# The start of an FFN's up projection: two operand copies moved from GpSimd to ScalarE, a new order of the last tile's steps, and the sample convolution cut into steps

## The chip, the cores and the metric

The kernel runs on one core of a Trainium2 chip. A core has five engines with a queue each: TensorE (PE, matrix products, with its weight loads shown as PEld), VectorE (DVE), ScalarE (ACT), GpSimd (POOL) and SyncE (SP, which only issues transfers here). They share an on-chip memory of 128 partitions (SBUF) and the accumulators that PE writes (PSUM). Each engine works through its own list in order and waits on semaphores for the others. The metric is the device time of one execution in microseconds; less is better.

## What is computed

One step of a one-layer hybrid encoder for 1024 prompt tokens and 32 sample tokens of a running stream, all in float32: a mixer with three kinds of heads, and behind it a feed-forward part with a short causal convolution. The change touches the first half of the feed-forward part.

```python
def causal_dwconv(x, buf, w, b):
    width, t = w.shape[0], x.shape[1]
    xp = jnp.concatenate([buf.astype(x.dtype), x], axis=1)
    y = b
    for j in range(width):
        y = y + xp[:, j:j + t] * w[j]
    return y, xp[:, t:]

def conv_ffn(xn, buf, w_up, conv_w, conv_b, w_down):
    up = xn @ w_up                                   # 1024 -> 2 * 2816
    up, buf = causal_dwconv(up, buf, conv_w, conv_b) # width 3
    gate, val = jnp.split(up, 2, axis=-1)
    return (jax.nn.gelu(gate, approximate=True) * val) @ w_down, buf

# in run_trunk, for the prompt and for the sample stream:
        x = x + rms_norm(h, g_mix_post[l])           # h: output projection of the mixer
        h, ffn_buf = conv_ffn(rms_norm(x, g_ffn_pre[l]), states[6][l], ffn_w_up[l], ffn_conv_w[l],
                              ffn_conv_b[l], ffn_w_down[l])
```

## The kernel before

**Products.** A float32 operand is kept as a high and a low half in PE's fp32r format, and each product is three matmuls, high x high, high x low and low x high (`mm3`, lines 88 to 90). The high half is made by an ACT cast, the low one by a DVE subtraction (`split`, line 94 and 97; `halves`, lines 1249 and 1250).

**Up projection.** The 22 feature tiles `f` hold 128 gate and 128 value columns each. A tile's product of 2 x 2 blocks (features x input rows against input rows x tokens) is done with seven block products instead of eight (`PROD`, `up_block`). Each goes with sums of weight blocks (A11, A12, A22 and S1 to S4, made for each tile by `up_operands`) and with sums of the normalised activations (B11, B21, B22, T1 to T4, made once by `col_operands`, from the blocks `xg` on lines 1258 to 1264, and kept for all tiles). A token block is 512 tokens wide. The results leave PSUM through ACT copies (`keep`, line 1333) and DVE sums into `uu` (line 1338); `up_finish` convolves `uu` (lines 1419 to 1425) and stores the product of both halves to `h_d`. Up to two tiles of `w_up` lie in `raw` buffers that the next loads reuse.

**The start.** The output projection of the mixer ends with token tiles 6 and 7 (`last[0]` and `last[1]`, generators of `outproj`). Their last steps, by `next`: add the norms' sums on POOL, scale, add the residual (DVE, lines 1167 to 1171), store, square (ACT, 1175), reciprocal root (POOL, 208 and 209), scale into `z` (ACT, 1178), and in the step behind it transpose `z` on PE (1195) and write it to `xg` with the column gains (DVE, 1199). Since these two tiles come late, tile 0 of the up projection is done in two halves: `s = 0` are the tokens of tiles 0, 1, 4 and 5, `s = 1` those of 2, 3, 6 and 7. The operands of `s = 0` are columns 0 to 255 of each operand tile, those of `s = 1` columns 256 to 511.

**Early places.** The tiles of T2 and T4 (pool `px1`) can only be laid where the output projection's weights (pool `p2`) have been. So T2 and T4 of `s = 0` are written first into the columns 256 to 511 of B22 and T1 (`early`), and copied to their own tiles afterwards by four instructions (line 1924). B22 and T1 of `s = 1` are written into the same columns behind these copies.

**Order.** A scheduler orders each engine's list by a simulated timeline and by priority, which is the order in which the instructions are issued in the code; `tc.high_priority(offset=n)` moves instructions up by `n` places. `with tc.issue_after(ins)` puts every instruction of the block that runs on the engine of `ins` behind `ins` in that engine's list. `kept` remembers instructions by name for this.

**Sample tokens.** The 32 sample tokens go through plain matmuls in 24 rounds of a 1 MB (for the last group 768 KB) load of `w_us` and 16 or 12 matmuls (`up_samples`, line 1452), in three groups of eight rounds with a transposition behind each group (lines 1463 and 1465). Two buffers `wus` take the loads. `up_all` steps this generator once for most tiles. The sample convolution (lines 1466 to 1476) runs on POOL on 128 x 704 elements, for the gate half into `smp_h` and for the value half into `smp_y`; its result is read only in the down projection.

**Pools.** Pools are stacked from both ends of SBUF: `px0` (B21, B11, T1, B22) on the left side, `p7` (`uu`, `fconv`, `pad1`, the `keep` tiles) and, opened after it and so next to it, `px1` (T3, T2, T4) on the right.

Of the kernel before, what the change touches and what calls it, by code (L numbers as in the profile page):

```python
# [8 lines left out]
F32 = mybir.dt.float32  # L9
# [3 lines left out]
AF = mybir.ActivationFunctionType  # L13
ALU = mybir.AluOpType
# [5 lines left out]
DEC = 32  # L20
# [58 lines left out]
def body(ctx: ExitStack, tc: tile.TileContext, a: dict):  # L79
# [988 lines left out]
    def outproj(p2, W, u):  # L1068
# [103 lines left out]
        sp.dma_start(x2_d[t0:t0 + n, :], x[:n])  # L1172
        if u == 7:
            z = tail[0]("z7")
        act.activation(z[:n], x[:n], AF.Square, accum_out=ss[:n, 0:1])
        rstd_of(ss[:n, 1:2], ss[:n, 0:1], n, 1, 1024)
        if u != 8:
            act.activation(z, x, AF.Copy, scale=ss[:, 1:2])
        else:
            dve.tensor_scalar(z[:n], x[:n], ss[:n, 1:2], None, op0=ALU.mult)  # L1180
        yield
# [49 lines left out]
    def col_operands(pool_, q, s, between=lambda: None, res=None, c=slice(None), parts="BTtq", at_=None):  # L1231

        res = {} if res is None else res
        q = {k: v[:, :, c] for k, v in q.items()}
        at = slice(256 * s + (c.start or 0), 256 * s + (c.stop or 256))

        def halves(name, src):
            if at_ and name in at_:
                h, l = at_[name]
            else:  # L1240
                if name not in res:
                    p = pool_[name in ("T2", "T4", "T3")]
                    res[name] = tuple(p.tile([128, 4, 512], F32R, name=f"{name}{x}") for x in "hl")
                h, l = (t[:, :, at] for t in res[name])
            with ExitStack() as late:
                if s == 0 and name in ("B21", "B11"):
                    late.enter_context(tc.issue_after(kept["ch"].ins))
                    late.enter_context(tc.issue_after(kept["cl"].ins))
                kept[name] = act.copy(h, src)
                return dve.tensor_tensor(l, src, h.bitcast(F32), op=ALU.subtract)  # L1250

        t1, t2, t3, t4 = q["B11"], q["B22"], q["B12"], q["B21"]
        if "B" in parts:
            halves("B21", t4)
            halves("B11", t1)
        if "T" in parts:
            between()
            dve.tensor_tensor(t1, t3, t1, op=ALU.subtract)
            halves("T1", t1)
            halves("B22", t2)  # L1260
        if "t" in parts:
            dve.tensor_tensor(t3, t2, t3, op=ALU.subtract)
            dve.tensor_tensor(t2, t2, t1, op=ALU.subtract)
            dve.tensor_tensor(t4, t2, t4, op=ALU.subtract)
            with ExitStack() as behind:
                if s == 0:
                    behind.enter_context(tc.issue_after(kept["jk"].ins))
                halves("T2", t2)
            kept["T4l"] = halves("T4", t4)
            between()  # L1270
        if "q" in parts:
            with tc.issue_after(kept["T4l"].ins), tc.issue_after(kept["T4"].ins), tc.issue_after(kept["T2"].ins):
                halves("T3", t3)
        return res
# [153 lines left out]
    def up_samples():  # L1428

        closing = ExitStack()  # L1430
        own = closing.enter_context(tc.tile_pool(name="pss", bufs=1, side="right", reuse_waits="tile"))

        def load(i):
            if i < len(ROUNDS):
                g, k = ROUNDS[i]
                nq = UGROUPS[g][1]
                sp.dma_start(wus[:, i % 2, :nq], a["w_us"][8 * g + k, :, :nq])

        smp_u = own.tile([128, NU, 2 + DEC], F32, name="smp_u")
        sp.dma_start(smp_u[:, :, 0:2], a["fcache"])  # L1440
        smp_y = [own.tile([128, NF, DEC], F32, name=f"smp_y{i}") for i in range(2)]
        smp_x = own.tile([128, 8, DEC], F32, name="smp_x")
        sp.dma_start(smp_x, xn_d[:, :, SEQ:])
        i = 0
        load(0)
        load(1)
        yield
        for g, (c0, nq) in enumerate(UGROUPS):
            ps = psf.tile([128, 512], F32, tag="sx", name=f"us{g}", bufs=1)
            for k in range(8):  # L1450
                for q in range(nq):
                    pe.matmul(ps[DEC * q:DEC * q + DEC], smp_x[:, k, :], wus[:, i % 2, q, :], start=k == 0, stop=k == 7)  # L1452
                load(i + 2)
                i += 1
                if k in (1, 3, 5):
                    yield
            m = DEC * nq
            us = own.tile([128, 512], F32, tag="us", name=f"usr{g}", bufs=1)
            act.copy(us[:m], ps[:m])
            yield  # L1460
            tp = psb.tile([128, 4, 128], F32, tag="big", name=f"ust{g}", bufs=3)
            for b in range(4):
                pe.transpose(tp[:, b, :m], us[:m, 128 * b:128 * b + 128], ident[:m, :m])
            for b in range(4):
                act.copy(smp_u[:, 4 * c0 + b:4 * (c0 + nq):4, 2:2 + DEC], tp[:, b, :m].rearrange("p (q t) -> p q t", t=DEC))
        pool.tensor_copy(fcq, smp_u[:, :, DEC:DEC + 2])
        for lo, dst in ((0, smp_h), (NF, smp_y[0])):
            js = slice(lo, lo + NF)
            w = [fconv[:, js, s:s + 1].broadcast_to([128, NF, DEC]) for s in range(4)]
            pool.tensor_tensor(dst, smp_u[:, js, 2:2 + DEC], w[2], op=ALU.mult)  # L1470
            pool.tensor_tensor(dst, dst, w[3], op=ALU.add)
            for s in range(2):
                pool.tensor_tensor(smp_y[1], smp_u[:, js, s:s + DEC], w[s], op=ALU.mult)
                pool.tensor_tensor(dst, dst, smp_y[1], op=ALU.add)
        act.activation(smp_h, smp_h, AF.Gelu_apprx_tanh)
        pool.tensor_tensor(smp_h, smp_h, smp_y[0], op=ALU.mult)
        closing.close()
        yield

    def up_all(pw_, W0, X, uus, py, freed, ahead, begun):  # L1480

        raw, W, summed = {}, {0: W0}, []
        late = None
        rounds = up_samples()
        n_rounds = 0
        for f in range(NF):
            uu = uus[f % len(uus)]
            if f + 1 < NF:
                raw[f + 1] = up_raw(f + 1)
            for s in (0, 1) if f == 0 else (None,):  # L1490
                if s != 0:
                    blk = up_block(pw_, f, s, W[f], X, uu)
                    next(blk)
                    next(late, None)
                    m = (2 * f + (1 if s is None else s) - 3) * len(SUMS) // 34
                    while len(summed) < min(m, len(SUMS)):
                        sum_weights(*SUMS[len(summed)])
                        summed.append(m)
                    if f:
                        up_finish(py(), f - 1, uus[(f - 1) % len(uus)])  # L1500
                        W.pop(f - 1)
                    next(blk)
                    if f == NF - 1:
                        freed()
                else:
                    blk = begun
                if s != 0 and f + 1 < NF:
                    ops = up_operands(f + 1, raw.pop(f + 1))
                    W[f + 1] = next(ops)
                    for _ in ops:  # L1510
                        pass
                yield
                while f and n_rounds < f * 15 // 17:
                    next(rounds, None)
                    n_rounds += 1
                next(blk)
                late = blk
                yield
        ahead()
        next(late, None)  # L1520
        up_finish(py(), NF - 1, uus[(NF - 1) % len(uus)])
# [2 lines left out]

    NP = NF // 2
    ROUNDS = [(g, k) for g in range(3) for k in range(8)]

    def sum_weights(t, n, q):

# [351 lines left out]
    uus[0] += [p7.tile([128, 2 + SEQ], F32, name=f"uu{j}") for j in range(2)]  # L1881
    for u in uus[0]:
        pool.memset(u[:, 0:2], 0.0)
    p7.tile([128, 8], F32, name="pad1")
    px1 = p8s.enter_context(tc.tile_pool(name="px1", bufs=1, side="right", reuse_waits="tile"))
    px.append(px1)
    col_operands(px, q0, 0, res=X, parts="q")
# [8 lines left out]
    wus = p3.tile([128, 2, 4, 512], F32, tag="xg0", name="wus", bufs=1)  # L1896
    py = []
    q1 = {f"B{k + 1}{j + 1}": (x1, xlate[1])[j][:, 4 * k:4 * k + 4, :] for k in range(2) for j in range(2)}
    with tc.high_priority(offset=10 * AHEAD), tc.issue_after(kept["T3"].ins):
        col_operands(px, q1, 1, res=X, parts="B")  # L1900
    with tc.high_priority(offset=10 * AHEAD):
        next(last[0])
        with tc.issue_after(kept["c1"].ins):
            next(last[1])
    begun = {}

    def freed():
# [11 lines left out]
    for i, _ in enumerate(up_all(pw_, W0, X, uus, lambda: py[0], freed, ahead, blk)):  # L1919
        if i == 1:  # L1920

            for n in ("T2", "T4"):
                for t, e in zip(X[n], early[n]):
                    pool.tensor_copy(t[:, :, :256], e)
            for x, c in zip(last, (slice(0, 128), slice(128, 256))):
                with tc.issue_after(done[0].ins), tc.issue_after(kept["c6"].ins):
                    next(x)
# [151 lines left out]
```

## Time and profile before

| | us |
|---|---|
| median of 3 runs | 1358.56 (1355.57 to 1362.2) |
| profiled execution | 1360.69 |
| its span | 1358.9 |
| PE busy | 1307.7 (96%) |
| DVE busy | 1018.0 (75%) |
| ACT busy | 693.8 (51%) |
| POOL busy | 316.2 (23%) |

A trace holds one execution; times in it count from the start of its span. A row of a timeline is start, duration, engine, line, operation, output tile <- input tiles, shapes and, in brackets, how long the engine had been idle and which instruction ended that. A row of the waits names who waited for whom, the sum, the count and the longest. A busy engine is not an engine at its peak: matmuls overlap, and the distance from one start to the next is what one costs. Tile 0 of the up projection runs from about 654 to 692 us, tile 21 ends near 1128.

### The profile page before, as it was taken

To read this page: it belongs to the slowest core of one execution; us is meant where nothing else is said; L and a number is where in the kernel's file an instruction comes from. 1 tells how busy PE (TensorE), PEld (TensorE's weight loads), DVE (VectorE), ACT (ScalarE), POOL (GpSimd) and SP (SyncE) were. 2 spreads that over 40 slices of the span, in tenths; PEclk is the share of its full clock that TensorE was granted. 3 is DMA by queue.
4 is the path that set the end of the run, shared out by engine and by line. 5 is a ranking of instruction groups with operands and counts; after the bars stand their busy time and mean duration, and the time that the engine had idled before them with its cause. 6 is when DMAs were issued, how large, how long until landed. Compare 5 with 4: busy or idle time off the path is not lost.

```text
span 1358.9 us, 25577 instructions
## 1 busy us (share of the span) xinstructions
PE 1307.7 (96%) x9896; PEld 1097.5 (81%) x9896; DVE 1018.0 (75%) x1748; ACT 693.8 (51%) x1294; POOL 316.2 (23%) x416
## 2 busy tenths in 40 slices
PE   6999999998999999999799999999999999999997
PEld 6999899998888977777788777877777886678885
DVE  5795659768598778865988777778789875399566
ACT  5555565464575556444555444544444444454552
POOL 4532312144031344232300101204023000010005
PEclk9999999999998999999999999999999999999999
DMA  9799879785889854444435888776864349644435
GB/s 342 241 356 368 275 242 286 267 284 180 295 253 326 307 202 131 145 144 159 128 129 171 236 246 220 199 220 184 243 157 116 102 159 358 242 159 131 148 111 123
DMA packets 134784, 291.73 MB, mean 215 GB/s; under 512 B 29015, under 2 KB 63991, under 8 KB 132535
## 3 DMA queue, kind: packets, MB, share of 16 engines
q1 hardware_dynamic: 121031, 267.03, 57.9%
q0 software_dynamic: 9120, 18.62, 7.6%
q10 hardware_dynamic: 4512, 4.46, 1.0%
q8 instruction: 77, 1.26, 0.4%
q14 instruction: 44, 0.36, 0.1%
HBM read 229.38 MB, written 85.78 MB: 232 GB/s over the span
## 4 chain that ended last, share of the span: by engine, by line
PE 57%; DVE 12%; ACT 3%; issue 2%; DMA 2%; POOL 1%; DVEq 0%; SPq 0%; POOLq 0%; ACTq 0%
PE pux_None L88 4%; PE pux_None L90 4%; PE pux_None L89 4%; PE puw_None L88 3%; PE puw_None L90 3%; PE puw_None L89 3%; PE q L88 2%; PE q L90 2%; PE q L89 2%; PE x L88 2%; PE x L89 2%; PE x L90 2%; PE us L1452 2%; PE zp L88 1%; PE zp L90 1%
## 5 line engine op out<-in xcount | busy, mean ns | idle before, releaser
L1422 DVE SCALAR_TENSOR_TENSOR y<-uu,fconv_sb,y 128x1024 f32<-128x1024 f32 x88 | 115.6, 1314 | 25.3 <-ACT y L1420 24.6
L1419 POOL COPY fhalo<-uu 128x2 f32<-128x2 f32 x44 | 17.6, 400 | 366.8 <-DVE uu L1338 355.0
L1420 ACT ACTIVATE y<-uu,fconv_sb 128x1024 f32<-128x1024 f32 x44 | 54.7, 1244 | 9.4 <-DVE uu L1338 8.9
L88 PE MATMUL pv<-wt_0h,xh 128*128 128x256 f32 (+1 forms) x192 | 56.5, 294 | 3.1 <-DVE xl L321 1.9
L90 PE MATMUL zp<-woh,cl 128*128 128x512 f32 (+1 forms) x144 | 57.6, 400 | 1.5 <-DVE cl L1093 1.5
L88 PE MATMUL zp<-woh,ch 128*128 128x512 f32 (+1 forms) x144 | 57.2, 406 | 0.8 <-ACT ch L1092 0.8
L89 PE MATMUL zp<-wol,ch 128*128 128x512 f32 (+1 forms) x144 | 57.6, 400 | 0.0
L90 PE MATMUL pv<-wt_1h,xl 128*128 128x256 f32 (+1 forms) x192 | 55.1, 287 | 0.0
L90 PE MATMUL pv<-wt_0h,xl 128*128 128x256 f32 (+1 forms) x192 | 54.9, 286 | 0.0
L88 PE MATMUL pv<-wt_1h,xh 128*128 128x256 f32 (+1 forms) x192 | 54.8, 286 | 0.0
L89 PE MATMUL pv<-wt_0l,xh 128*128 128x256 f32 (+1 forms) x192 | 54.7, 285 | 0.0
L89 PE MATMUL pv<-wt_1l,xh 128*128 128x256 f32 (+1 forms) x192 | 54.5, 284 | 0.0
L1655 POOL TENSOR_TENSOR gss<-gss 128x1 f32<-128x1 f32 (+1 forms) x9 | 9.2, 1021 | 186.8 <-ACT gjk L1648 186.8
L208 POOL TENSOR_SCALAR hrs<-hss 128x5 f32<-128x5 f32 (+3 forms) x27 | 10.1, 374 | 174.2 <-DVE hss L1002 169.6
L818 DVE COPY_PREDICATED P<-masks_sb,sc 128x352 f32<-128x352 int32 (+3 forms) x53 | 37.8, 714 | 5.8 <-PE sc L731 5.2
L88 PEld LDWEIGHTS pv<-wt_0h,xh 128*128 128x128 f32 x192 | 36.3, 189 | 5.3 <-DVE xl L321 2.4
L1424 ACT ACTIVATE y<-y 128x1024 f32<-128x1024 f32 x22 | 23.3, 1059 | 27.7 <-DVE y L1422 27.7
L88 PEld LDWEIGHTS pv<-wt_1h,xh 128*128 128x128 f32 x192 | 36.3, 189 | 0.7 <-issue 0.6
L209 POOL TENSOR_TENSOR hrs<-hrs,mhalf 128x5 f32<-128x5 f32 (+3 forms) x27 | 36.2, 1341 | 2.3
L89 PEld LDWEIGHTS pv<-wt_0l,xh 128*128 128x128 f32 x192 | 36.4, 190 | 0.2
L90 PEld LDWEIGHTS pv<-wt_0h,xl 128*128 128x128 f32 x192 | 36.4, 189 | 0.2
L90 PEld LDWEIGHTS pv<-wt_1h,xl 128*128 128x128 f32 x192 | 36.1, 188 | 0.3
(1898 smaller groups left out, 4679.0 us busy)
## 6 DMA issues: line engine op xcount, KB each, us to landing
wus<-in_w_us SPq DMA_DIRECT2D x16, 1024.0 KB, 6.5
wrP<-in_w_dn SPq DMA_DIRECT2D x27, 512.0 KB, 4.9
h_d<-y SPq DMA_DIRECT2D x22, 512.0 KB, 5.8
ht<-h_d SPq DMA_DIRECT2D x22, 512.0 KB, 9.5
wt_0r<-in_w_tok SPq DMA_DIRECT2D x21, 512.0 KB, 5.3
wt_1r<-in_w_tok SPq DMA_DIRECT2D x21, 512.0 KB, 6.1
ws_d<-in_w_dn POOLq DMA_DIRECT2D x20, 512.0 KB, 7.2
wrP<-ws_d SPq DMA_DIRECT2D x20, 512.0 KB, 4.1
```

Of the source, the lines that this page charges most:

```text
L88: pe.matmul(ps, lh[0], rh[0], start=first, stop=False, **kw)
L89: pe.matmul(ps, lh[0], rh[1], start=False, stop=False, **kw)
L90: return pe.matmul(ps, lh[1], rh[0], start=False, stop=last, **kw)
L208: pool.tensor_scalar(out, ss, 1.0 / width, eps, op0=ALU.mult, op1=ALU.add)
L209: pool.tensor_tensor(out, out, mhalf[:n, :cols], op=ALU.pow)
L818: dve.copy_predicated(dst, mk.broadcast_to([n, 11, *mk.shape[2:]]), src)
L1419: behind["POOL"] = pool.tensor_copy(fhalo[:, j, :], u[:, SEQ - 2:SEQ])
L1420: act.activation(y, u, AF.Identity, scale=fconv[:, j, 2:3], bias=fconv[:, j, 3:4])
L1422: dve.scalar_tensor_tensor(y, uu[i][:, s:s + SEQ], fconv[:, j, s:s + 1], y, op0=ALU.mult, op1=ALU.add)
L1424: act.activation(ys[0], ys[0], AF.Gelu_apprx_tanh)
L1452: pe.matmul(ps[DEC * q:DEC * q + DEC], smp_x[:, k, :], wus[:, i % 2, q, :], start=k == 0, stop=k == 7)
L1655: pool.tensor_tensor(ss[:n, 0:1], ss[:n, 2:3], ss[:n, 3:4], op=ALU.add)
```

## The change

- The four copies of T2 and T4 are ACT copies instead of POOL copies, put behind the scaling `z` of token tile 7 (`kept["z"]`).
- The steps of token tiles 6 and 7 are issued ahead of the B operands of `s = 1`. Tile 7's step stands behind `t4`, the DVE instruction of line 1264, as well as behind `c1`; the B operands stand behind the square of tile 7 as well as behind T3's cast.
- `up_samples` is stepped once for each tile from tile 1 on, and once more for each tile after the twelfth. The convolution has a `yield` before each POOL instruction. The ring and the visits get names and keep their values.
- `pad1` in `p7` has 40 elements a partition instead of 8.

```diff
-        act.activation(z[:n], x[:n], AF.Square, accum_out=ss[:n, 0:1])
+        kept["sq"] = act.activation(z[:n], x[:n], AF.Square, accum_out=ss[:n, 0:1])
...
-            act.activation(z, x, AF.Copy, scale=ss[:, 1:2])
+            kept["z"] = act.activation(z, x, AF.Copy, scale=ss[:, 1:2])
...
-            dve.tensor_tensor(t4, t2, t4, op=ALU.subtract)
+            kept["t4"] = dve.tensor_tensor(t4, t2, t4, op=ALU.subtract)
...
         i = 0
-        load(0)
-        load(1)
-        yield
+        for i in range(RING_S):
+            load(i)
+        yield
+        i = 0
...
             w = [fconv[:, js, s:s + 1].broadcast_to([128, NF, DEC]) for s in range(4)]
+            yield
             pool.tensor_tensor(dst, smp_u[:, js, 2:2 + DEC], w[2], op=ALU.mult)
+            yield
             pool.tensor_tensor(dst, dst, w[3], op=ALU.add)
             for s in range(2):
+                yield
                 pool.tensor_tensor(smp_y[1], smp_u[:, js, s:s + DEC], w[s], op=ALU.mult)
+                yield
                 pool.tensor_tensor(dst, dst, smp_y[1], op=ALU.add)
+        yield
         act.activation(smp_h, smp_h, AF.Gelu_apprx_tanh)
         pool.tensor_tensor(smp_h, smp_h, smp_y[0], op=ALU.mult)
         closing.close()
-        yield
...
                 yield
-                while f and n_rounds < f * 15 // 17:
+                if f:
                     next(rounds, None)
-                    n_rounds += 1
                 next(blk)
                 late = blk
+                if f > len(UGROUPS) * (len(VISITS) + 1):
+                    next(rounds, None)
                 yield
+        for _ in rounds:
+            pass
...
+    RING_S, VISITS = 2, (1, 3, 5)
...
-    p7.tile([128, 8], F32, name="pad1")
+    p7.tile([128, 40], F32, name="pad1")
...
-    with tc.high_priority(offset=10 * AHEAD), tc.issue_after(kept["T3"].ins):
-        col_operands(px, q1, 1, res=X, parts="B")
     with tc.high_priority(offset=10 * AHEAD):
         next(last[0])
-        with tc.issue_after(kept["c1"].ins):
+        with tc.issue_after(kept["c1"].ins), tc.issue_after(kept["t4"].ins):
             next(last[1])
+    with tc.high_priority(offset=10 * AHEAD), tc.issue_after(kept["T3"].ins), tc.issue_after(kept["sq"].ins):
+        col_operands(px, q1, 1, res=X, parts="B")
...
-            for n in ("T2", "T4"):
-                for t, e in zip(X[n], early[n]):
-                    pool.tensor_copy(t[:, :, :256], e)
+            with tc.issue_after(kept["z"].ins):
+                for n in ("T2", "T4"):
+                    for t, e in zip(X[n], early[n]):
+                        act.copy(t[:, :, :256], e)
```

More of the change, by code (lines that the diff above doesn't have):

```diff
@@ L1436, in load @@
                 nq = UGROUPS[g][1]
-                sp.dma_start(wus[:, i % 2, :nq], a["w_us"][8 * g + k, :, :nq])
+                sp.dma_start(wus[:, i % RING_S, :nq], a["w_us"][8 * g + k, :, :nq])
         smp_u = own.tile([128, NU, 2 + DEC], F32, name="smp_u")
@@ L1451, in up_samples @@
                 for q in range(nq):
-                    pe.matmul(ps[DEC * q:DEC * q + DEC], smp_x[:, k, :], wus[:, i % 2, q, :], start=k == 0, stop=k == 7)
-                load(i + 2)
+                    pe.matmul(ps[DEC * q:DEC * q + DEC], smp_x[:, k, :], wus[:, i % RING_S, q, :], start=k == 0, stop=k == 7)
+                load(i + RING_S)
                 i += 1
-                if k in (1, 3, 5):
+                if k in VISITS:
                     yield
@@ L1484, in up_all @@
         rounds = up_samples()
-        n_rounds = 0
         for f in range(NF):
```

## The prediction

> **What bounds the kernel now.** I read the page first, then PE's waits between 640 and 1128 us (the stage that the diff touches), then busy time by window, then the timelines of the engines named there.
>
> ```profile
> span 1358.9 us, 25577 instructions
> PE 57%; DVE 12%; ACT 3%; issue 2%; DMA 2%; POOL 1%; DVEq 0%; SPq 0%; POOLq 0%; ACTq 0%
> ```
>
> PE holds most of the chain that ended last, so a gain has to come from PE's gaps or from PE's own speed. PE's waits in the stage are these, of 0.5 us and more:
>
> ```profile
> PE fxt L1195 <- ACT z L1178: 3.3, 1, 3.3
> PE puy L89 <- DVE B21l L1250: 1.3, 1, 1.3
> PE pux_None L88 <- ACT c_17None L1333: 1.1, 1, 1.1
> PE puw L89 <- DVE T1l L1250: 0.9, 1, 0.9
> PE puz L88 <- ACT T1h L1249: 0.9, 1, 0.9
> PE puy_None L88 <- ACT A_18h L94: 0.6, 1, 0.6
> ```
>
> Two places, and nothing between them. The rows without `_None` belong to tile 0, which runs in two halves of 256 tokens: 3.3 + 1.3 + 0.9 + 0.9 = 6.4 us. The two with `_None` lie at tile 17 to 18: 1.7 us. The windows show what the first place costs beside idle time:
>
> ```profile
> 670.00:675.00 5.00, 1.71 (x15) 1.51 (x15) 4.34 (x9) 2.98 (x5) 0.00 (x0) 1.00 0.50 211
> 675.00:680.00 5.00, 4.06 (x20) 3.76 (x20) 4.93 (x8) 2.11 (x4) 0.00 (x0) 0.52 0.62 9
> 680.00:685.00 5.00, 5.00 (x25) 4.38 (x24) 3.94 (x6) 2.67 (x4) 0.00 (x0) 0.80 0.00 0
> 720.00:820.00 100.00, 100.00 (x459) 77.72 (x458) 77.08 (x100) 47.70 (x70) 10.90 (x16) 1.00 0.74 214
> 1008.00:1040.00 32.00, 30.33 (x134) 24.28 (x133) 29.92 (x28) 13.26 (x23) 18.49 (x13) 1.00 0.47 111
> 1120.00:1128.00 8.00, 8.00 (x36) 6.38 (x34) 5.23 (x7) 3.92 (x6) 0.18 (x1) 1.00 1.03 419
> ```
>
> The columns are length, busy time of PE, weight loads, DVE, ACT and POOL, granted clock, DMA share and GB/s. Behind PE's long wait the clock is granted at 0.52 and 0.80 for ten microseconds: (0.48 + 0.20) x 5 = 3.4 us of PE speed gone. From 720 on PE is full at clock 1.00 and DVE is busy 77%: there only faster matmuls would help.
>
> **Part 1: order and engine of the start of tile 0.** The chain goes through DVE:
>
> ```profile
> 656.51 1.42 DVE L1167 SCALAR_TENSOR_TENSOR zp<-zp,oss,gm 128x512 f32<-128x512 f32 x2 [1.12 <-POOL oss L209]
> 657.83 1.22 DVE L1264 TENSOR_TENSOR xg<-xg 128x1024 f32<-128x1024 f32 x1
> 660.49 1.46 DVE L1250 TENSOR_TENSOR B22l<-xg,B22h 128x1024 fp32r<-128x1024 f32 x1
> 665.83 2.05 DVE L1250 TENSOR_TENSOR B21l<-xg,B21h 128x1024 fp32r<-128x1024 f32 x1
> 667.80 1.21 DVE L1250 TENSOR_TENSOR B11l<-xg,B11h 128x1024 fp32r<-128x1024 f32 x1
> 677.89 0.69 DVE L1250 TENSOR_TENSOR T1l<-xg,T1h 128x512 fp32r<-128x512 f32 x1
> 664.78 2.02 POOL L1924 CAST T4l<-T1l 128x1024 fp32r<-128x1024 f32 x1
> 668.01 1.41 POOL L209 TENSOR_TENSOR oss<-oss,mhalf 128x1 f32<-128x1 f32 x1
> ```
>
> Putting the last tile's steps behind `t4` (L1264) lets that 1.22 us instruction into the 1.12 us in which DVE waited for POOL: 1.1 us. The four subtractions from 660.49 to 667.80 take 7.31 us beside POOL's copies (the last of them the CAST at 664.78); the next one, with POOL quiet, takes 1.21, so four take 4.84: 2.5 us. Together DVE comes 3.6 us earlier to the subtraction at 677.89, which is the one that PE's last wait is for.
>
> The copies go to ACT, so ACT has to have room:
>
> ```profile
> 662.09 1.05 ACT L1249 CAST B21h<-xg 128x1024 fp32r<-128x1024 f32 x1
> 663.04 1.04 ACT L1249 CAST B11h<-xg 128x1024 fp32r<-128x1024 f32 x1
> 663.98 1.06 ACT L1175 ACTIVATE z<-xr 128x1024 f32<-128x1024 f32 x1
> 670.97 0.62 ACT L1249 CAST B22h<-xg 128x512 fp32r<-128x512 f32 x1 [5.57 <-DVE xg L1199]
> 672.79 1.15 ACT L1178 ACTIVATE z<-xr,oss 128x1024 f32<-128x1024 f32 x1
> 676.14 0.62 ACT L1249 CAST T1h<-xg 128x512 fp32r<-128x512 f32 x1 [2.20 <-DVE xg L1258]
> 678.63 0.58 PE L89 MATMUL puw<-T1l,S_0h 128*128 128x256 f32 x1 [0.94 <-DVE T1l L1250]
> 681.14 0.63 PE L88 MATMUL pux_None<-B11h,A_1h 128*128 128x512 f32 x1
> ```
>
> A copy of 1024 columns starts 0.95 us after the one before it, so four are 3.8 us of ACT. They stand behind the scaling `z`, and the casts into the same columns (B22h at 670.97) stand behind them, with PE and DVE waiting for those casts. ACT idled 5.57 us there; when DVE comes 3.6 us earlier, 2.0 us are left, and copies plus `z` (moved from 672.79 to before them) need 4.9. So B22h comes at 670.97 - 3.6 + 2.9 = 670.3. Three more short instructions stood between it and `z`, 1.8 us in all; then T1h of the last tile can go at about 672, against 676.14: 4 us, the same as DVE allows. The square (663.98) waited behind B21h and B11h and its POOL step (668.01) behind the copies; ahead of both, `z` is no longer late and PE's 3.3 us wait for it goes. What is late next is T1l again: with some of DVE's short pauses filled I take 3.9 us for PE's start at 678.63, to 674.7. The twelve matmuls there now take 681.14 - 678.63 = 2.5 us at about half clock. At full clock they would save about 1.2 us. PE still has one gap of about 3 us in front of them, so I count half of that: **4.5 us** for the start. Bounds: nothing at all, if ACT's casts come no earlier, and 6.4 + 3.4 = 9.8 if gap and clock loss both vanish.
>
> [...]
>
> **Part 2: the sample work.** The visits of the up projection go from 15 in 17 tiles to one each tile; the same matmuls, copies and loads are issued. A load in SP's queue waits for the ring slot that its matmuls free, and the next `w_up` loads queue behind it; rival 4 prices that. The convolution is cut into single POOL instructions:
>
> ```profile
> 928.87 1.69 POOL L1470 TENSOR_TENSOR smp_h<-smp_u,fconv_sb 128x704 f32<-128x704 f32 x1 [5.58 <-ACT smp_u L1465]
> 1015.16 1.90 POOL L1470 TENSOR_TENSOR smp_y<-smp_u,fconv_sb 128x704 f32<-128x704 f32 x1
> 1028.75 2.05 POOL L1476 TENSOR_TENSOR smp_h<-smp_h,smp_y 128x704 f32<-128x704 f32 x1
> 1017.54 1.90 DVE L1304 TENSOR_TENSOR wu17r<-wu39r,wu17r 128x512 f32<-128x512 f32 x1
> ```
>
> Seven of them stand from 1015.16 to 1028.75, and DVE's 128x512 instructions beside them take 1.90 in place of 0.69: 1.2 us each, 8.4 in all. PE lost 1.7, so about 6.7 us of DVE's delay are hidden in a tile. Spread at two a tile, 2.4 us would be hidden whole: 1.7 us gained. But the first half's six ran from 928.87, as soon as ACT had written their input, although the code issues both halves in one step, of which the second half ran 86 us later. Issue order did not hold them back, and I see no new edge in the diff that would. So I expect two bursts again, earlier by some tiles, and take **0** out of 0 to 1.7.
>
> **Part 3: `pad1`.** It grows from 32 to 160 bytes a partition, which moves all of `px1` (T3, T2, T4) down by 128 bytes; B11, B21, B22 and T1 lie on the other side and stay. In the allocation of the kernel before, the first start 128 bytes past a multiple of 256, the others and the `w_up` halves on one. Products of twelve matmuls each:
>
> ```profile
> 1002.34 0.40 PE L88 MATMUL pux_None<-T3h,S_15h 128*128 128x512 f32 x1
> ...
> 1005.13 0.39 PE L89 MATMUL pux_None<-B11l,A_16h 128*128 128x512 f32 x1
> ...
> 1007.64 0.39 PE L88 MATMUL puw_None<-T1h,S_16h 128*128 128x512 f32 x1
> ...
> 1010.36 0.40 PE L88 MATMUL puz_None<-T4h,A_16h 128*128 128x512 f32 x1
> ...
> 1013.15 0.49 PE L1463 MATMUL ust<-ident,usr 96*128 96x96 f32 x4
> ```
>
> T3's takes 2.79 us, T1's 2.72, T4's 2.79. Three such products in 21 tiles: 63 x 0.07 = 4.4 us of PE, in a stretch where PE never waits. Bounds are 0 (placement has nothing to do with it) and 4.4; the other way it can go as far again, but the new residue is that of T1, whose row is the fast one. I take **3.7**, as not every product need be slowed that much.
>
> [...]
>
> **Sum**: 4.5 + 0 + 3.7 = 8.2 us. The profiled execution took 1360.69 us (span 1358.9), so 1352.5; the median of the runs, 1358.56, lies 2.1 below it, so **1350.4**.
>
> **Rivals.**
> 1. The clock stays full: the start gives 4.5 + 0.6 and the first matmuls of tile 1 another 0.6, 5.7 in all: 1349.2. For it: the gap is shorter than the one that did it. Against it: barely.
> 2. Placement does nothing: 4.5 alone, 1354.1. For it: the difference is 0.07 in 2.7 and could belong to neighbours' traffic. Against it: T3 and T4 write to different banks and at different points of the tile, and both show it.
> 3. ACT takes POOL's place: if the copies are not done when DVE has its input ready, B22h and T1h come no earlier, and the start gives 0.5: 1358.56 - 0.5 - 3.7 = 1354.4. For it: ACT is filled from 662 to 673 by the sum above. Against it: it idled 5.57 + 2.20 us before.
> 4. Slower: the sample loads, now without pauses, hold the `w_up` loads behind them in SP's queue in tiles 2 to 13. It decides where these come over 6.7 us late. One microsecond beyond costs 12 tiles x 1 = 12: 1358.56 - 8.2 + 12 = 1362.4, and two make 1374. Against it: DMA share is 0.74 at 214 GB/s, and 419 GB/s were moved at 1120.
>
> **How the numbers follow.** Forecast 0.42 (alone 1347 to 1353.5), rival 1 0.20, rival 2 0.18, rival 3 0.14, rival 4 0.06. Half a per cent, about what a measurement of this kernel can tell from no change, is 6.8 us: below 1351.8 or above 1365.4. The forecast lies 1.4 us beyond that line and rival 1 2.6, so I give faster about two thirds of the first, nine tenths of the second, and a quarter of rivals 2 and 3, where the convolution's 1.7 comes in after all: 0.28 + 0.18 + 0.08 = 0.54. Slower by that much is most of rival 4: 0.05. The rest, 0.41, is within. The range leaves out rival 4 and reaches from 1344.5 (start 8, all of the convolution, 4.4 of placement) to 1357.5 (rival 2 or 3 with little of the rest).
>
> **What would show it.** POOL has no CAST in tile 0, ACT has four more, and DVE's subtractions there take 1.2 us. PE's wait for `z` is gone; its wait for T1l ends by 675. If ACT's casts of B22h and T1h come after 673, it is rival 3. T2's, T3's and T4's products take 2.72 us (rival 2: 2.79). The POOL products stand in two rows of six or seven, or in pairs. Waits of PE for `A` or `S` operands in tiles 2 to 13 would be rival 4. A reordering of the instruction lists outside this stage would make the whole sum wrong.

## The result and the profile after

| | before | after |
|---|---|---|
| median, us | 1359.12 (22 runs, 1354.39 to 1362.2) | 1353.93 (22 runs, 1349.37 to 1361.03) |
| ratio | | 0.9964 (95% interval 0.9951 to 0.9976) |
| profiled execution, its span | 1360.69, 1358.9 | 1354.02, 1351.2 |
| granted clock of the profiled execution | 0.988 | 0.985 |

The change is worth 1359.12 x 0.0036 = 4.9 us (3.3 to 6.7). All comparisons below leave out two slow runs of the kernel before, of 1599.71 and 2124.28 us, whose granted clock was 0.75 and 0.557. From the profile page of the changed kernel, the chain of work that ended last:

```profile
PE 61%; DVE 8%; ACT 2%; DMA 2%; issue 2%; POOL 1%; DVEq 0%; SPq 0%; POOLq 0%; ACTq 0%
```

PE holds more of the chain than before (57%). PE's waits in the same stage, 656 to 712 us, where the columns are total, count and longest:

```profile
PE puw L88 <- ACT T1h L1249: 2.5, 1, 2.5
PE puw L89 <- DVE T1l L1250: 1.1, 1, 1.1
PE puz L88 <- ACT T1h L1249: 0.6, 1, 0.6
PE pux L88 <- ACT B22h L1249: 0.4, 1, 0.4
```

The wait of 3.3 us for `z` is gone, and so are the two at tiles 17 and 18: from 712 to the end of tile 21 no wait of PE for another engine is left. But a new wait of 2.5 us for T1h stands where `z` stood. Since the two profiles reach the up projection at different times, distances are taken from the last product of the output projection (`zp`). The timeline of PE before, that product and the first one of the down projection:

```profile
654.10 0.40 PE L90 MATMUL zp<-woh,cl 128*128 128x512 f32 x1
...
1117.74 0.39 PE L88 MATMUL q<-P2w,P2h 128*128 128x512 f32 x1
```

and the same two after:

```profile
656.56 0.40 PE L90 MATMUL zp<-woh,cl 128*128 128x512 f32 x1
...
1112.07 0.39 PE L88 MATMUL q<-P2w,P2h 128*128 128x512 f32 x1
```

The stage takes 463.64 us before and 455.51 after: 8.1 us less, nearly the forecast's 8.2. The whole program gained 4.9. The experiments show what each part did to the stage, and what the stage's gain was worth in the end.

**The start after.** The timeline of the changed kernel, DVE, POOL, ACT and PE one after the other:

```profile
657.87 1.23 DVE L1264 TENSOR_TENSOR xg<-xg 128x1024 f32<-128x1024 f32 x1
659.82 1.42 DVE L1167 SCALAR_TENSOR_TENSOR zp<-zp,oss,gm 128x512 f32<-128x512 f32 x2 [0.72 <-POOL oss L209]
...
668.41 1.22 DVE L1250 TENSOR_TENSOR B11l<-xg,B11h 128x1024 fp32r<-128x1024 f32 x1
...
674.42 0.69 DVE L1250 TENSOR_TENSOR B22l<-xg,B22h 128x512 fp32r<-128x512 f32 x1 [1.00 <-ACT B22h L1249]
...
678.62 0.69 DVE L1250 TENSOR_TENSOR T1l<-xg,T1h 128x512 fp32r<-128x512 f32 x1
...
658.10 1.05 POOL L208 TENSOR_SCALAR oss<-oss 128x1 f32<-128x1 f32 x1
...
668.93 1.15 ACT L1178 ACTIVATE z<-xr,oss 128x1024 f32<-128x1024 f32 x1 [0.49 <-POOL oss L209]
669.99 1.03 ACT L1933 CAST T2h<-B22h 128x1024 fp32r<-128x1024 f32 x1
...
672.83 1.04 ACT L1933 CAST T4l<-T1l 128x1024 fp32r<-128x1024 f32 x1
673.77 0.61 ACT L1249 CAST B22h<-xg 128x512 fp32r<-128x512 f32 x1
...
675.60 0.61 ACT L1249 CAST T1h<-xg 128x512 fp32r<-128x512 f32 x1
...
676.26 0.38 PE L88 MATMUL puw<-T1h,S_0h 128*128 128x256 f32 x1 [2.45 <-ACT T1h L1249]
...
679.37 0.58 PE L89 MATMUL puw<-T1l,S_0h 128*128 128x256 f32 x1 [1.09 <-DVE T1l L1250]
```

`t4` (L1264) does run in DVE's pause. But POOL's root step for the last tile, which DVE waits for in the pause, has to run beside it now, and its first instruction takes 1.05 us. Before, it ran while DVE was idle:

```profile
655.64 0.19 POOL L208 TENSOR_SCALAR oss<-oss 128x1 f32<-128x1 f32 x1
```

So the step behind it, L1167, starts 659.82 - 656.56 = 3.26 us after the last `zp`, against 656.51 - 654.10 = 2.41. The pause was lengthened by 0.85 us, and 0.72 of idle time is left in it. The subtractions do take 1.22 us without POOL's copies. Together the last of them, B11l, ends 13.07 us after `zp` in place of 14.91, 1.8 us earlier and not 3.6. Then ACT is late: four copies from 669.99 to 673.87 stand between `z` and the casts. DVE idles 1.00 us for B22h, and PE waits 2.45 us for T1h.

**The clock after.** Windows of 3.41 us, laid on the edges of the recorded clock steps; the columns are those of the windows in the prediction. After:

```profile
673.49:676.90 3.41, 0.70 (x4) 0.30 (x2) 2.48 (x5) 3.41 (x8) 0.00 (x0) 1.00 1.06 113
676.90:680.31 3.41, 2.17 (x6) 1.45 (x7) 3.41 (x8) 0.62 (x2) 0.00 (x0) 0.50 0.11 2
680.31:683.73 3.42, 3.42 (x14) 3.03 (x13) 3.35 (x4) 1.61 (x3) 0.00 (x0) 0.50 0.00 0
```

and before:

```profile
671.81:675.22 3.41, 1.23 (x11) 1.23 (x12) 3.08 (x6) 2.13 (x4) 0.00 (x0) 0.99 0.21 87
675.22:678.63 3.41, 2.47 (x13) 2.17 (x12) 3.34 (x6) 2.11 (x4) 0.00 (x0) 0.50 0.72 11
678.63:682.05 3.42, 3.42 (x14) 3.23 (x15) 2.61 (x4) 0.67 (x2) 0.00 (x0) 0.51 0.18 3
```

In both, a window with PE busy for 0.70 or 1.23 us of 3.41 is followed by two windows at half clock. The shorter wait didn't spare the clock.

**Placement.** The starts of the products in the changed kernel:

```profile
1019.59 0.39 PE L88 MATMUL pux_None<-T3h,S_16h 128*128 128x512 f32 x1
...
1022.31 0.39 PE L88 MATMUL pux_None<-B11h,A_17h 128*128 128x512 f32 x1
...
1025.03 0.39 PE L88 MATMUL puw_None<-T1h,S_17h 128*128 128x512 f32 x1
...
1027.75 0.39 PE L88 MATMUL puz_None<-T4h,A_17h 128*128 128x512 f32 x1
```

T3's product takes 2.72 us, as B11's and T1's do; it took 2.79.

**Convolution.** It is still two bursts, as forecast. First and last instruction of each:

```profile
889.28 1.76 POOL L1472 TENSOR_TENSOR smp_h<-smp_u,fconv_sb 128x704 f32<-128x704 f32 x1 [4.29 <-ACT smp_u L1466]
...
900.41 1.71 POOL L1479 TENSOR_TENSOR smp_h<-smp_h,smp_y 128x704 f32<-128x704 f32 x1
...
961.00 1.41 POOL L1472 TENSOR_TENSOR smp_y<-smp_u,fconv_sb 128x704 f32<-128x704 f32 x1
...
974.66 2.04 POOL L1482 TENSOR_TENSOR smp_h<-smp_h,smp_y 128x704 f32<-128x704 f32 x1
```

The second one lies some 54 us earlier than before, and no wait of PE stands beside it this time.

### The profile page after: what moved, and what is told of

The parts are those of the page before. It is cut to its first block, busy times and chain, and to the rows that moved or that the text cites. A ratio compares the mean times of both kernels' runs of the same rounds, so it can differ in the third digit from the quotient of the medians.

```text
span 1351.2 us, 25580 instructions
## 1 busy us (share of the span) xinstructions
PE 1306.0 (97%) x9896; PEld 1100.5 (81%) x9896; DVE 1012.7 (75%) x1748; ACT 696.9 (52%) x1298; POOL 310.3 (23%) x412
## 4 chain that ended last, share of the span: by engine, by line
PE 61%; DVE 8%; ACT 2%; DMA 2%; issue 2%; POOL 1%; DVEq 0%; SPq 0%; POOLq 0%; ACTq 0%
PE pux_None L88 4%; PE pux_None L90 4%; PE pux_None L89 4%; PE q L88 3%; PE puw_None L89 3%; PE puw_None L88 3%; PE puw_None L90 3%; PE q L89 3%; PE q L90 3%; PE x L88 2%; PE x L89 2%; PE x L90 2%; PE us L1453 2%; PE zp L88 2%; PE zp L90 2%
## 5 line engine op out<-in xcount | busy, mean ns | idle before, releaser
L1419 POOL COPY fhalo<-uu 128x2 f32<-128x2 f32 x44 | 17.2, 391 | 362.8 <-DVE uu L1338 351.2
L208 POOL TENSOR_SCALAR hrs<-hss 128x5 f32<-128x5 f32 (+3 forms) x27 | 11.1, 412 | 175.1 <-DVE hss L1002 172.8
L89 PEld LDWEIGHTS pv<-wt_1l,xh 128*128 128x128 f32 x192 | 36.2, 189 | 0.1
```

The lines of the kernel that those rows point to most:

```text
L89: pe.matmul(ps, lh[0], rh[1], start=False, stop=False, **kw)
L208: pool.tensor_scalar(out, ss, 1.0 / width, eps, op0=ALU.mult, op1=ALU.add)
L1419: behind["POOL"] = pool.tensor_copy(fhalo[:, j, :], u[:, SEQ - 2:SEQ])
```

## The experiments

Each kernel ran beside the kernel before on the same chip. The stage is the distance from the last `zp` product to the first product of the down projection, in its one profile. The last column is (1 - granted clock) x span, the mean over its runs with the standard error: the clock time that was not granted in the whole program.

| kernel | median, us (runs) | ratio to before, 95% | stage, us | lost to half clock, us |
|---|---|---|---|---|
| before | 1359.2 to 1360.6 (94) | | 463.6 | 17.1 ± 0.3 |
| after | 1353.93 (22) | 0.9951 to 0.9976 | 455.5 | 19.4 ± 0.5 |
| e1_pad | 1353.63 (6) | 0.9936 to 0.9969 | 459.5 | 14.7 ± 1.2 |
| e2_start | 1359.66 (12) | 0.9996 to 1.0035 | 462.3 | 19.1 ± 0.9 |
| e3_sample | 1359.46 (12) | 0.9978 to 1.0005 | 461.5 | 18.2 ± 0.6 |
| e4_no_pad | 1357.95 (12) | 0.9964 to 0.9996 | 460.2 | 18.9 ± 0.8 |
| e5_no_start | 1353.22 (12) | 0.9927 to 0.9972 | 457.3 | 17.0 ± 1.0 |
| e6_t4_free | 1354.53 (11) | 0.9934 to 0.9967 | 455.5 | 14.9 ± 0.6 |
| e7_t1_first | 1351.52 (6) | 0.9921 to 0.9962 | 453.6 | 19.4 ± 0.6 |
| e8_both | 1350.62 (6) | 0.9899 to 0.9950 | 452.3 | 15.1 ± 1.5 |
| e9_left | 1355.77 (12) | 0.9958 to 0.9986 | 458.1 | 17.2 ± 0.7 |
| e10_pad24 | 1360.97 (12) | 0.9988 to 1.0023 | 462.7 | 18.8 ± 1.0 |
| e11_again | 1353.93 (12) | 0.9947 to 0.9977 | 455.7 | 18.6 ± 0.8 |
| e12_start_new | 1355.38 (12) | 0.9957 to 0.9995 | 458.7 | 14.5 ± 0.9 |

The stage of a profile holds the clock loss of that one execution. There it is 3.4 us in before, after, e1 to e4, e10 and e11, 1.7 in e5, e7 and e9, and none in e6, e8 and e12. So the stages of e5 to e9 and e12 differ from before and after by their clock too.

### One part at a time: e1 to e4

The kernel before with one part of the diff each. e1_pad:

```diff
-    p7.tile([128, 8], F32, name="pad1")
+    p7.tile([128, 40], F32, name="pad1")
```

e2_start has the new names in `kept`, the new order and the ACT copies:

```diff
-    with tc.high_priority(offset=10 * AHEAD), tc.issue_after(kept["T3"].ins):
-        col_operands(px, q1, 1, res=X, parts="B")
...
-        with tc.issue_after(kept["c1"].ins):
+        with tc.issue_after(kept["c1"].ins), tc.issue_after(kept["t4"].ins):
             next(last[1])
+    with tc.high_priority(offset=10 * AHEAD), tc.issue_after(kept["T3"].ins), tc.issue_after(kept["sq"].ins):
+        col_operands(px, q1, 1, res=X, parts="B")
...
-                    pool.tensor_copy(t[:, :, :256], e)
+                        act.copy(t[:, :, :256], e)
```

e3_sample has the changes in `up_samples` and `up_all`:

```diff
-                while f and n_rounds < f * 15 // 17:
+                if f:
                     next(rounds, None)
-                    n_rounds += 1
...
+            yield
             pool.tensor_tensor(dst, smp_u[:, js, 2:2 + DEC], w[2], op=ALU.mult)
```

e4_no_pad is the changed kernel with the old pad:

```diff
-    p7.tile([128, 40], F32, name="pad1")
+    p7.tile([128, 8], F32, name="pad1")
```

> The kernel before with pad1 of 40 elements, nothing else. Theory (placement): T2, T3 and T4 now start on the same residue modulo 256 as the weight halves; their products take 2.72 us like T1's and not 2.79, PE gains 3.5 to 4 us between 692 and 1124, ratio 0.9971 to 0.9974. PE's waits at tile 0 (6.4 us) and at tile 17 to 18 (1.7 us) stay. Rival (placement does nothing, the faster products of the changed kernel come from less traffic): 2.79 as before, ratio 1.000.

> The kernel before with the new order of the last tile's steps and the four copies on ACT, nothing else. Theory: as in the changed kernel the wait for z goes and waits of 2.5 and 1.1 us for T1h and T1l come in its place, the clock still falls; 1.5 to 2 us gained, ratio 0.9985 to 0.9989. Rival (the start gives the 4.5 us that were forecast, and something else in the changed kernel takes it back): ratio 0.9967.

> The kernel before with the sample visits once a tile and the convolution cut into steps, nothing else. Theory: the convolution still runs in two bursts, three tiles earlier, and the second one falls where tile 13 or 14 hides it; PE's two waits at tile 17 to 18 (1.7 us) go: ratio 0.9988. Rival (the bursts cost PE as much wherever they lie): 1.000.

> The changed kernel with pad1 back at 8 elements. Theory (parts add up): start and sample work alone, 3.2 to 3.7 us, ratio 0.9973 to 0.9976, and T2's to T4's products at 2.79 us again. Rival (placement is not additive, or nothing): as the changed kernel, 0.9964.

In the stage the parts add up: 463.6 less 4.1 (pad), 1.3 (start) and 2.1 (sample) is 456.1; the change has 455.5. The kernel without the pad has 460.2, which is the start's and the sample's gains together. The pad leaves every wait of before in place, the first of them here in the waits of e1_pad:

```profile
PE fxt L1195 <- ACT z L1178: 3.3, 1, 3.3
```

So its gain comes from the products' own speed. In whole times the pad shows more than its 4.1 us and the start nothing: 1.0015 is 2.0 us slower, with an interval from 0.5 faster to 4.8 slower. Both miss what was expected of them. The loss to the half clock points the same way, 14.7 us in e1 and 19.1 in e2 against 17.1 before; as e1 has the start of before, its low loss in six runs may be chance.

### What the start costs, and a better one: e5 to e8

All four are the changed kernel with an edit. e5_no_start undoes what e2 does; two of its places:

```diff
-        with tc.issue_after(kept["c1"].ins), tc.issue_after(kept["t4"].ins):
+        with tc.issue_after(kept["c1"].ins):
...
-                        act.copy(t[:, :, :256], e)
+                    pool.tensor_copy(t[:, :, :256], e)
```

e6_t4_free takes away one rule:

```diff
-        with tc.issue_after(kept["c1"].ins), tc.issue_after(kept["t4"].ins):
+        with tc.issue_after(kept["c1"].ins):
```

e7_t1_first reorders ACT's copies and casts (parts "1" is T1's share of parts "T", parts "2" that of B22), and e8_both has the edits of e6 and e7:

```diff
-                for n in ("T2", "T4"):
-                    for t, e in zip(X[n], early[n]):
-                        act.copy(t[:, :, :256], e)
+                for t, e in zip(X["T4"], early["T4"]):
+                    act.copy(t[:, :, :256], e)
...
-                col_operands(px, q1, 1, res=X, c=c, parts="T")
+                col_operands(px, q1, 1, res=X, c=c, parts="1")
+            with tc.issue_after(kept["T1"].ins):
+                for t, e in zip(X["T2"], early["T2"]):
+                    act.copy(t[:, :, :256], e)
+            for c in (slice(0, 128), slice(128, 256)):
+                col_operands(px, q1, 1, res=X, c=c, parts="2")
```

> The changed kernel with the start of the pass put back: POOL copies T2 and T4, the order of the squares and of t4 as before; the new placement and the spread visits of the sample stay. Theory A (the reordered start saves work but costs clock: its PE waits of 2.5, 0.4 and 1.1 us lie within 6 us of one another, and the kernels that have it lost about 19.2 us to the half clock, those without 16.9): about 1335.1 us of work at full clock (1341.4 before, less 4.1 and 2.2 of the two single parts) plus 16.9, so about 1352 to 1354, no slower than the changed kernel. Theory B (that difference in lost clock is chance): the start is worth its 2.1 us whole, so the changed kernel (1353.9) plus 2.1, about 1356. Either way the waits of the start are those of the kernel before (POOL root step 3.3, then 1.3, 1.1) and the waits on the sample at tiles 17 and 18 are gone.

> The changed kernel without the rule that DVE's t4 goes ahead of the last tile's scaling chain. Theory (t4 in the pause slows POOL's tiny root step beside it from 0.19 to 1.05 us, which puts the whole chain 0.85 us later): the root step for the last tile takes 0.2 us again, the first PE wait on T1h shrinks from 2.5 to about 1.7 us, but t4's 1.1 us comes back ahead of the T1l products, so the wait on them stays at 1 to 2 us; time within 1 us of the changed kernel. Rival (the root step is slow for another reason, so t4's place costs nothing): root step still about 1 us, and t4 behind the chain makes the wait on T1l 1.1 us longer, time about 1 us up.

> The changed kernel with ACT's start in the order of need: T4's copies, T1's two casts, then T2's copies, then B22's casts. Theory (ACT is now what ends last at the start: its four copies of about 0.9 us and two B22 casts of 0.8 stand ahead of T1h): T1h's second half about 2 us earlier against the last zp product, the PE waits of 2.5 and 1.1 us together down by 1.5 to 2.5 us, so 1 to 2.5 us of work less than the changed kernel, and with shorter gaps about 1 us less lost to the half clock: about 1351.5. Rival (DVE's T1l products behind its own column work are what PE waits for, whatever ACT does): the wait on T1h goes over to T1l and the time stays within 0.7 us of the changed kernel.

> The last two together: t4 not ahead of the scaling chain, and ACT's copies in the order of need. Theory (both the root step and the order of ACT's copies set the end of the start): T1h's second half 2.5 to 3 us earlier against the last zp product than in the changed kernel, and about 1350.5 us. Rival (DVE's own work ends last): no better than the one with ACT's order alone.

Without the start (e5) the time is no worse than with it: ratios 0.9949 and 0.9964. Its stage is 1.8 us longer and its loss to the clock 2.4 us less, as theory A had it; the difference of the times alone is within the intervals and decides nothing.

With `t4` free, POOL's step is short again, in the timeline of e6_t4_free:

```profile
660.32 0.19 POOL L208 TENSOR_SCALAR oss<-oss 128x1 f32<-128x1 f32 x1
```

PE's largest waits there:

```profile
PE puz L88 <- ACT T1h L1249: 0.9, 1, 0.9
PE pux L88 <- ACT T2h L1249: 0.8, 1, 0.8
PE puw L89 <- DVE T1l L1250: 0.6, 1, 0.6
```

The wait of 2.5 us is split up, and the loss to the clock falls from 19.4 to 14.9 us. But the time stays where it was, and so does the stage: a wait for T2h is new, and the 112 sample products of the next 180 us take 14.9 us from start to start in place of 13.0, since two of their rounds of 16 matmuls were split by other products. With T1 before T2 alone (e7), T1h and T1l are waited for 1.0 and 1.4 us, and the clock still falls: the loss stays at 19.4 us, where 1 us less was expected. Only both together (e8) do better than the change: 0.9924 (0.9899 to 0.9950), 10.3 us less than before in six runs. Its largest waits:

```profile
PE puz L88 <- ACT T1h L1249: 0.9, 1, 0.9
PE puw L89 <- DVE T1l L1250: 0.8, 1, 0.8
```

and its emptiest window in that place, at full clock and followed by full clock:

```profile
675.25:678.66 3.41, 2.03 (x13) 1.63 (x13) 3.41 (x7) 3.41 (x7) 0.00 (x0) 1.00 1.02 56
678.66:682.07 3.41, 3.21 (x13) 2.32 (x14) 3.41 (x6) 1.71 (x4) 0.00 (x0) 1.00 0.01 0
```

e5, whose start is that of before, has windows on both sides of a half:

```profile
678.27:681.68 3.41, 1.74 (x15) 1.75 (x16) 3.38 (x7) 1.61 (x3) 0.00 (x0) 1.00 0.05 19
681.68:685.10 3.42, 1.70 (x12) 1.30 (x11) 3.38 (x6) 2.01 (x4) 0.00 (x0) 1.00 0.90 13
685.10:688.51 3.41, 3.41 (x14) 3.02 (x14) 2.75 (x6) 1.60 (x3) 0.00 (x0) 0.50 0.00 0
```

A window with PE busy 1.74 us was followed by full clock, one with 1.70 by half. Other windows at the start of tile 0 lie the same way: those with 0.67 (e11), 0.70 (after), 1.10 (e10), 1.12 (e7) and 1.23 us (before) were followed by half clock, those with 2.03 (e8), 2.14 (e12) and 2.22 (e6) by full. It is no rule for the whole program, as two windows of the kernel before show:

```profile
586.44:589.85 3.41, 1.63 (x11) 1.06 (x10) 3.41 (x9) 1.62 (x4) 1.86 (x4) 1.00 0.43 150
589.85:593.27 3.42, 2.76 (x93) 2.63 (x94) 3.35 (x9) 0.00 (x0) 0.00 (x0) 1.00 0.46 162
```

Here 1.63 us were followed by full clock. At 494.28 a window with PE busy for 3.25 us, in 54 matmuls of which 52 are only 64 columns wide, was followed by half. What the clock counts is open.

### What makes a product slow: e9 and e10

Both are the kernel before with an edit. e9_left, ahead of the `w_up` halves in their pool:

```diff
+    p4.tile([128, 32], F32, name="padl")
```

e10_pad24:

```diff
-    p7.tile([128, 8], F32, name="pad1")
+    p7.tile([128, 24], F32, name="pad1")
```

> The kernel before with one unused tile of 128 bytes per partition ahead of the column pass's weights, nothing else: the weight halves and the moving halves B and T1 move from a multiple of 256 bytes to one of 128 only, and T2, T3 and T4 stay where they are, on an odd multiple of 128. Theory (a product is slow when the starts of its moving and its stationary operand differ modulo 256 bytes): all products now agree, every one takes 227 ns, and about 4 us go, as with the first placement run: about 1355.5. Rival (the moving operand has to start on a multiple of 256, whatever the weights do): now all of the pass's products take 232, the T halves as before and the B halves with them, and the time goes up by 3 to 5 us.

> The kernel before with the pad ahead of the T halves at 24 elements instead of 8: T2, T3 and T4 start at 64 or 192 modulo 256 bytes, the weights at 0. Theory (any difference modulo 256 is slow): T2 to T4 products at about 232 ns as before, time the same within 0.3%. Rival (only an offset of 128 is slow, or multiples of 64 suffice): 227 ns and 4 us less. A third outcome, slower than 232, would say that finer misplacement costs more.

e9 leaves T2 to T4 where they were slow, and moves the weights and B and T1 instead. PE's timeline of e9_left:

```profile
1018.95 0.39 PE L88 MATMUL pux_None<-T3h,S_16h 128*128 128x512 f32 x1
...
1021.67 0.39 PE L88 MATMUL pux_None<-B11h,A_17h 128*128 128x512 f32 x1
...
1024.39 0.39 PE L88 MATMUL puw_None<-T1h,S_17h 128*128 128x512 f32 x1
...
1027.11 0.39 PE L88 MATMUL puz_None<-T4h,A_17h 128*128 128x512 f32 x1
```

All of them take 2.72 us, and 3.8 us go (0.9972). So it isn't where the moving operand starts alone: by the allocation, all fast products here have both operands on the same remainder modulo 256 bytes, and moving either side by 128 does it. The rival's 3 to 5 us more are out. A moving operand at 0 against weights at 128 was not run, so that weights at 128 are always fast is not excluded. With the remainders 64 apart (e10) the time is that of before, and the products are slow again, but not the same ones:

```profile
1019.97 0.40 PE L88 MATMUL pux_None<-T3h,S_16h 128*128 128x512 f32 x1
...
1022.74 0.40 PE L88 MATMUL pux_None<-B11h,A_17h 128*128 128x512 f32 x1
...
1025.51 0.39 PE L88 MATMUL puw_None<-T1h,S_17h 128*128 128x512 f32 x1
...
1028.23 0.40 PE L88 MATMUL puz_None<-T4h,A_17h 128*128 128x512 f32 x1
```

T3's and B11's take 2.77, T1's 2.72. B11 wasn't moved. Why the product behind T3's is slow there stays open.

By placement alone, PE took 2.79 us a product for T3 in before and 2.72 in e9.

### The start again, and the better start alone: e11 and e12

e11 is the changed kernel unchanged. e12_start_new is the kernel before with e8's start, and neither pad nor sample work; against e2 it has the edits of e6 and e7:

```diff
-        with tc.issue_after(kept["c1"].ins), tc.issue_after(kept["t4"].ins):
+        with tc.issue_after(kept["c1"].ins):
...
+            with tc.issue_after(kept["T1"].ins):
+                for t, e in zip(X["T2"], early["T2"]):
+                    act.copy(t[:, :, :256], e)
```

> The changed kernel as it is, for a second profile and more times beside the same runs of the kernel before. Theory (its start always puts PE's waits of 2.5, 0.4 and 1.1 us close together, and the clock answers): the stretch of half clock some 20 us behind the last zp product is there again, the mean loss to the half clock again about 19 us. Rival (that stretch was chance in the one profile): absent or elsewhere, loss near the 17 us of the kernels without the reordered start.

> The kernel before with the better start alone (copies of T2 and T4 on ACT in the order of need, B1 and B21's products with the square first, no rule for t4), the old placement and the old sample visits. Theory (the start was worth about 4 us and the change lost it to t4's place, to the order of ACT's copies and to the half clock): about 1356, with no half clock in the 30 us behind the last zp product. Rival (the start is worth nothing in any order, and the gain of the last two kernels together is chance of their few runs): 1359 to 1360, as the change's start alone.

e11's profile has the same waits (2.4 and 1.4 us) and the same two windows at half clock, behind this one:

```profile
670.26:673.67 3.41, 0.67 (x2) 0.47 (x3) 2.92 (x6) 3.41 (x8) 0.00 (x0) 1.00 1.11 111
```

e12 has no half clock there, loses 14.5 us to it in the whole program, and takes 0.9976 (0.9957 to 0.9995) of the time of before, 3.3 us less, where the change's start alone (e2) took nothing off. So the start did hold a gain about as large as forecast (0.7 to 5.8 us by the interval), in another order.

By kind of start, over all runs: the old start loses 17.2 ± 0.2 us to the half clock (148 runs), the change's order 19.1 ± 0.4 (after, e2, e4, e11; 58 runs), the order with `t4` free 14.7 ± 0.5 (e6, e8, e12; 29 runs). Between runs of one kernel, a microsecond more of this loss goes with 0.82 ± 0.04 us more time (241 runs, with e7's six). As an estimate, the change's start gives back 1.9 x 0.82 = 1.6 us on average. The losses are those of whole runs; that the differences arise at the start is read from the single profiles.

## Why the prediction was right, and where it wasn't

The forecast was 1350.4 us in a range from 1344.5 to 1357.5; the median is 1353.93. The saving came to 0.36%, in the direction that was forecast but short of the half per cent that the prediction took as its line and gave 0.54 to pass.

| term | forecast | the part alone, in the stage | the part alone, by ratio |
|---|---|---|---|
| start | 4.5 | 1.3 | -2.0 (-4.8 to 0.5) |
| convolution | 0 | 2.1 | 1.1 (-0.7 to 3.0) |
| placement | 3.7 | 4.1 | 6.5 (4.2 to 8.7); 3.8 by e9 |
| sum | 8.2 | 7.5 | change: 4.9 (3.3 to 6.7) |

**Placement: right**, mechanism and size. 2.79 us became 2.72, and of the bound of 4.4 us some 4 came. Rival 2 is out.

**Start: the step that failed.** Most of what was to be seen was seen: no POOL cast, ACT's four copies, 1.22 us subtractions, no wait for `z`. PE's wait for T1l did not end by 675. Four sentences of the prediction's Part 1 were wrong.

- "Putting the last tile's steps behind `t4` (L1264) lets that 1.22 us instruction into the 1.12 us in which DVE waited for POOL: 1.1 us." The pause wasn't free: what DVE waited for in it was a POOL instruction that took 1.05 us beside `t4` in place of 0.19. L1167 came 0.85 us later, and e6 shows the 0.19 us again with that one rule gone.
- "Together DVE comes 3.6 us earlier": 1.8 at B11l.
- "Then T1h of the last tile can go at about 672." In the time of that profile, which ran 2.46 us late, it went at 675.60 - 2.46 = 673.14, 3.0 us earlier in place of 4. ACT's copies stood in front of it, which was half of rival 3: in the same time the first B22h cast came at 673.77 - 2.46 = 671.31, no earlier than before (670.97), and T1h only just behind the rival's mark of 673. Behind T1h, DVE's own work held T1l until 678.62. PE's wait for it ended at 679.37 - 2.46 = 676.91, 1.7 us earlier than before and not 3.9.
- "PE still has one gap of about 3 us in front of them, so I count half of that", 0.6 us of clock gained. The gap was shorter (2.45 us) and the clock fell just the same: with the other waits beside it, PE was busy for 0.70 us of the window. By the estimate above the new order lost 1.6 us more on average. With the stage's 1.3 us gained, the start nets nothing, and that is what e2 and e5 measure.

Rival 1 (the clock stays full) did not come here. It came in e6, e8 and e12, whose starts have another order. In none of the windows of 3.41 us given above for the start of tile 0 was PE idle throughout: in front of half clock it was busy for 0.67 (e11) to 1.70 us (e5). The recorded clock steps lie on a grid: in the traces of before and after, the time from one step to the next is always a whole multiple of 3.413 us. With the old start the half clock lasts 6.8 us in three profiles (before, e1, e3) and 3.4 in three (e5, e9, e10); what decides between the two was not shown. With the change's start it lasts 6.8 in all four (after, e2, e4, e11), but in these the emptiest window begins 17 to 17.5 us behind the last `zp` each time, so other positions of the grid were not seen.

**Convolution: the bursts were right, the 0 was the wrong end of its bounds.** Both bursts came earlier, and the second left PE no wait; e3 alone loses the waits of 1.1 and 0.6 us. Why DVE's delay is covered there and was not around 1020 us is not shown. Rival 4 didn't come: from tile 2 on PE waits for no operand.

**The sum.** In the stage it was nearly right by compensation: start 3.2 too much, convolution 2.1 and placement 0.4 too little. Of the 8.1 us that the stage gained, 3.2 are missing in the whole time. By the estimate above 1.6 of them went to the clock; the other 1.6 lies within the error of the times and of one pair of profiles, and stays open.

## What to carry to other kernels

- Before filling an engine's pause, look at what the pause waits for: if that instruction takes longer beside the filler (here 1.05 us in place of 0.19), the pause moves with it.
- Where the clock falls at a start, look at how empty the emptiest short window is, not only at the longest wait: here several waits of 0.9 us cost less than one of 2.5 with another close behind.
- When products of one shape differ by 2 to 3% by operand, compare where both operands start: here a pad of 128 bytes was worth about 4 us, and the reordered start nothing by itself.

## What the runs showed of the hardware that was not expected

- Matmuls of 128 x 512 in fp32r followed each other at 2.72 / 12 = 0.227 us where, by the allocation, moving and stationary operand start on the same remainder modulo 256 bytes (0 and 0 for T1 in before, 128 and 128 for T3 in e9), and at 2.79 / 12 = 0.233 with the moving one at 128 and the stationary one at 0 (T3 in before). In e10 B11's at 0 and 0, behind T3's, took 2.77 / 12 = 0.231.
- A POOL instruction on 128 x 1 elements (L208) took 0.19 us while DVE was idle (before) and 1.05 beside a DVE subtraction of two SBUF tiles (after); there it ended at 659.15, just behind that one (657.87 + 1.23 = 659.10).
- At the start of tile 0 the clock fell to half behind windows of 3.41 us in which PE was busy for 0.67 (e11) to 1.70 us (e5), and not behind those with 1.74 (e5) or 2.03 (e8) to 2.22 (e6). It stayed there for another window when the next one had 2.07 (e11) to 2.47 (before), and not with 2.68 (e10) or 3.21 (e7). Elsewhere in the program busy time does not part the windows in this way: in before 1.63 us were followed by full clock and 3.25 by half.
